# Seven-product block multiplication kept for the gate half only, and the weight sums on VectorE instead of GpSimd, in a two-layer streaming trunk

## The chip, the core and the metric

The kernel runs on one core of a Trainium2 chip. The core has five engines with a queue each: TensorE (PE in the profile; its weight loads are PEld), VectorE (DVE), ScalarE (ACT), GpSimd (POOL) and SyncE (SP), which here only issues DMAs. The metric is the device time of one execution in microseconds (us). The kernel before takes 935.57 us, the median of three runs (935.47 to 936.04). A difference under about 0.2% (2 us) can hardly be told from no change by such a measurement.

## The reference, cut to what is touched

Two residual layers work on a sequence of 512 tokens of width 1024. The first (mLSTM heads beside stick-breaking attention) isn't touched. The second, cut:

```
def odd_layer(x, pre_g, post_g, w_in, pool_w, pool_scale, w_out):
    h = rmsnorm(x, pre_g)
    u = h @ w_in                                  # 512 x 1024 times 1024 x 4096
    p, z = u[..., :2048], u[..., 2048:]           # pooled half, gate half
    pooled = multiscale_pool(p.reshape(B, S, 4, 512))   # trailing mean over 2/4/8/16 tokens, minus the token
    mixed = einsum('bsgc,gce->bsge', pooled, pool_w)    # one 512 x 512 map per group
    y = (mixed.reshape(B, S, 2048) * pool_scale * silu(z)) @ w_out
    return x + rmsnorm(y, post_g)
```

## The kernel before, in words

**Number format.** Every matmul runs in float32r, and each operand is split in two parts, high (`ACT` copies it rounded, line 71) and low (`VectorE` subtracts, line 72). A product of two operands takes three matmuls (`mm3`, lines 95 to 97): high by high, low by high, high by low. So each weight tile costs ScalarE and VectorE one instruction, whatever it is multiplied with. Names that begin with `wh` and `wl` are the two parts of a weight tile.

**The second layer** runs over four channel groups `g` of 512 channels with windows 2, 4, 8, 16. For each group: (1) the pooled half `p`: four channel blocks of 128 (`cur4`), from two weight loads of 1024 x 256; (2) for each of the four blocks the trailing sums by repeated shift and add on VectorE (line 762, once for window 2, up to four times for window 16), a correction of the first tokens on GpSimd (lines 767 and 768, a few columns), the subtraction of the token (line 769), and the split (`pph`, `ppl`); (3) the gate half `z`, two weight loads, with SiLU (`sz`); (4) the map `pool_w`: 48 matmuls into `mx`, and the product with `sz` (line 791).

**Seven products.** Except for `p` of group 0, which is projected directly, every load of 1024 x 256 weights goes through `strassen2`. It sees the weights as four blocks (two halves of the inner dimension by two output blocks) and the transposed hidden state as four blocks too (two halves of the inner dimension by two halves of the sequence). Seven products of such blocks give the four blocks of the result where the plain way takes eight. Each is 4 inner tiles by 3 matmuls, 128 x 256 in shape: 84 matmuls a call. The price is additions: four sums of weight blocks (`s1` to `s4` in the tiles `ws0`, `ws1`; 128 x 512 each), written by GpSimd; four sums of hidden blocks, once for the kernel (`hidden_sums`: `d3`, `d1`, `n2`, `t4`); and partial results that ScalarE copies out of PSUM (`pt`) and VectorE adds (lines 717, 723, 725). The split tiles are `a` (the plain blocks of the first output column), `b` (`s2`, `s1`), `c` (`s3`, `s4`) and `d` (one plain block). `project2` is the plain way: for each of two channel blocks 8 inner tiles by 3 matmuls of 128 x 512, 48 a call, with two split tiles of 128 x 1024.

**What sets the order.** The program is handed to a scheduler that orders each engine's queue by its own estimate of times; each queue then runs strictly in that order. Pools bound how far a stage can run ahead: `wh` and `wl` have four buffers, the raw weights `w32` two, `ws` three, the PSUM tag `pj` two banks (the `psa` of `strassen2`, the `ps` of `project2`), `xa` and `xb` one each (`psb`, `pse`), `ac` two (`mx`).

Of the kernel before, what the change touches and what calls it, by code (L numbers as in the profile page):

```python
# [7 lines left out]
AF = mybir.ActivationFunctionType  # L8
ALU = mybir.AluOpType
# [27 lines left out]
def body(nc, tc, x, pre_g, post_g, w_in, conv, b_i, b_f, hn_g, w_out, w_in_c, pool_w,  # L37
         pool_scale, w_out_c, out):
    V, A, G, T = nc.vector, nc.scalar, nc.gpsimd, nc.tensor
# [4 lines left out]
    with base as base, psum as psum, dram as dram:  # L44
# [25 lines left out]
        def split(src, hi, lo):  # L70
            A.activation(hi, src, AF.Copy)  # L71
            V.tensor_tensor(lo, src, hi.bitcast(F32), op=ALU.subtract)  # L72

        def whl(name):
            return (base.tile([P, WIDE], F32R, tag="wh", bufs=4, name=f"wh_{name}"),
                    base.tile([P, WIDE], F32R, tag="wl", bufs=4, name=f"wl_{name}"))
# [9 lines left out]
        def halves(w, name, into=None):  # L86

            a, n = w.shape[1], w.shape[2]
            wh, wl = (t[:, :a * n].rearrange("p (a n) -> p a n", a=a) for t in (into or whl(name)))
            split(w, wh, wl)  # L90
            return wh, wl
# [94 lines left out]
        def col_load(src, name):  # L186

            w = load(lambda t: [(nc.sync, t, src)], 8, 256, name)
            return [lambda i=i: halves(w[:, :, i * P:i * P + P], f"{name}_{i}") for i in range(2)]
# [6 lines left out]
        def project2(src, name):  # L196
            for i, w in enumerate(col_load(src, name)):
                ps = pj(f"ps_{name}_{i}")
                col_proj(w(), ps)
                yield ps  # L200

        with tc.tile_pool(name="att", bufs=1) as at:
# [386 lines left out]
            for h in range(HA):  # L589
# [7 lines left out]
                for s in range(NB):  # L597
                    t = bc[:, ROW[s]:ROW[s] + P]
# [28 lines left out]
        with tc.tile_pool(name="odd", bufs=1) as od:  # L627
# [60 lines left out]
            def strassen2(src, name, dsts, silu=False):  # L688

                w = load(lambda t: [(nc.sync, t, src)], 8, 256, name)  # L690
                a11, a12, a21, a22 = (w[:, 4 * k:4 * k + 4, m * P:m * P + P]
                                      for m in range(2) for k in range(2))
                sums = [ws(f"ws{i}_{name}") for i in range(2)]
                s1, s2, s3, s4 = sums[0][:, 4:], sums[0][:, :4], sums[1][:, :4], sums[1][:, 4:]
                G.tensor_tensor(s1, a21, a22, op=ALU.add)  # L695
                G.tensor_tensor(s2, s1, a11, op=ALU.add)
                G.tensor_tensor(s3, a11, a21, op=ALU.add)
                G.tensor_tensor(s4, a12, s2, op=ALU.add)
                first = halves(w[:, :, :P], f"{name}_a")
                second = halves(sums[0], f"{name}_b")  # L700
                third = halves(sums[1], f"{name}_c")
                fourth = halves(a22, f"{name}_d")

                def product(ps, wt, k0, b, start, stop):
                    (wh, wl), (bh, bl) = wt, hs[b]
                    for k in range(4):
                        mm3(ps, (wh[:, k0 + k], wl[:, k0 + k]), (bh[:, k], bl[:, k]),
                            start and k == 0, stop and k == 3, skip_group_check=True)

                def part(i): return od.tile([P, 256], F32, tag="part", bufs=4, name=f"pt{i}_{name}")  # L710

                pa, pb, pe = (f(f"ps{n}_{name}")[:, :256] for f, n in ((pj, "a"), (xa, "b"), (xb, "e")))
                t1, t2, t5 = part(1), part(2), part(5)
                product(pa, first, 0, "11", True, True)
                A.activation(t1, pa, AF.Copy)
                product(pb, first, 4, "21", True, True)
                V.tensor_tensor(dsts[0][:, :256], pb, t1, op=ALU.add)
                product(pa, second, 0, "n2", False, True)
                A.activation(t2, pa, AF.Copy)
                product(pe, second, 4, "d1", True, True)  # L720
                A.activation(t5, pe, AF.Copy)
                product(pa, third, 0, "d3", False, True)
                V.scalar_tensor_tensor(dsts[1][:, 256:], pa, -1.0, t5, op0=ALU.mult, op1=ALU.subtract)
                product(pe, third, 4, "22", False, True)
                V.tensor_tensor(dsts[0][:, 256:], pe, t2, op=ALU.add)
                product(pa, fourth, 0, "t4", False, True)
                if silu:
                    act(dsts[0], dsts[0], AF.Silu)
                    act(dsts[1][:, 256:], dsts[1][:, 256:], AF.Silu)
                    act(dsts[1][:, :256], pa, AF.Silu, scale=-1.0)  # L730
                else:
                    A.activation(dsts[1][:, :256], pa, AF.Copy, scale=-1.0)

            for g, w in enumerate(WINDOWS):
                pooled = []
                cur4 = []
                for j in range(4):
                    c = 4 * g + j
                    cur = od.tile([P, 16 + S], F32, tag="win", bufs=6, name=f"p_{c}")
                    G.memset(cur[:, :16], 0.0)  # L740
                    cur4.append(cur)
                wsrc = [w_in_c[0, :, 512 * g + 256 * i:512 * g + 256 * i + 256] for i in range(2)]
                if g == 0:
                    wj = [t() for i in range(2) for t in col_load(wsrc[i], f"p{g}{i}")]
                    for j, n0 in ((j, n0) for n0 in (0, 256) for j in range(4)):
                        ps = pj(f"ps_p{4 * g + j}_{n0}")
                        col_proj(wj[j], ps, n0, n0 + 256)
                        A.activation(cur4[j][:, 16 + n0:16 + n0 + 256], ps[:, n0:n0 + 256], AF.Copy)
                    hidden_sums()
                else:  # L750
                    for i in range(2):
                        strassen2(wsrc[i], f"p{g}{i}", [t[:, 16:] for t in cur4[2 * i:2 * i + 2]])
                for j in range(4):
                    c = 4 * g + j
                    cur = cur4[j]
                    p32 = cur[:, 16:]
                    sh = 1
                    while sh < w:
                        nx = od.tile([P, 16 + S], F32, tag="win", bufs=6, name=f"p_{c}_{sh}")
                        if 2 * sh < w:  # L760
                            G.memset(nx[:, :16], 0.0)
                        V.tensor_tensor(nx[:, 16:], cur[:, 16:], cur[:, 16 - sh:16 + S - sh],  # L762
                                        op=ALU.add)
                        cur, sh = nx, 2 * sh
                    sm = cur[:, 16:]
                    e = w - 1
                    G.tensor_tensor(sm[:, :e], sm[:, :e], invc[:, :e], op=ALU.mult)
                    G.tensor_tensor(sm[:, :e], sm[:, :e], p32[:, :e], op=ALU.subtract)
                    V.scalar_tensor_tensor(sm[:, e:], sm[:, e:], 1.0 / w, p32[:, e:], op0=ALU.mult,
                                           op1=ALU.subtract)  # L770
                    ph = od.tile([P, S], F32R, tag="phi", bufs=5, name=f"pph{c}")
                    pl = od.tile([P, S], F32R, tag="plo", bufs=5, name=f"ppl{c}")
                    split(sm, ph, pl)
                    pooled.append((ph, pl))
                sz = []
                for i in range(2):
                    pair = [od.tile([P, S], F32, tag="sz", bufs=4, name=f"sz{4 * g + 2 * i + j}")
                            for j in range(2)]
                    strassen2(w_in_c[0, :, 2048 + 512 * g + 256 * i:2304 + 512 * g + 256 * i],
                              f"z{g}{i}", pair, True)  # L780
                    sz.extend(pair)
                w4 = load(lambda t: [(nc.sync, t, pool_w[0, g])], 4, 512, f"pw{g}")
                pw = [halves(w4[:, 2 * i:2 * i + 2], f"pw{g}{i}") for i in range(2)]
                for e in range(4):
                    c = 4 * g + e
                    ps = ac(f"mx{c}")
                    for k in range(4):
                        wh, wl = pw[k // 2]
                        mm3(ps, (wh[:, k % 2, e * P:e * P + P], wl[:, k % 2, e * P:e * P + P]),
                            pooled[k], k == 0, k == 3)  # L790
                    V.scalar_tensor_tensor(y32[:, c], ps, psc(c), sz[e], op0=ALU.mult, op1=ALU.mult)
# [44 lines left out]
```

## Time and profile before

| | |
|---|---|
| median of three runs | 935.57 us (935.47 to 936.04) |
| the profiled execution: its own time, its span | 938.04 us, 936.3 us |
| PE busy | 903.9 us, 97% of the span |
| VectorE busy | 603.9 us, 65% |
| ScalarE busy | 503.3 us, 54% |
| GpSimd busy | 170.4 us, 18% |
| mean granted PE clock | 0.981 |

The second layer's groups lie between about 605 and 845 us of the span; then follows the output projection. In the timeline an instruction's duration for PE is that of a pipelined one, from issue to its modelled end; what a matmul costs in a row of them is the distance between two starts. The same holds for VectorE, where a 128 x 512 addition shows 0.68 us and the next one starts 0.60 us after it. A group of instructions is named by line, engine, and output<-inputs, without buffer numbers.

### The profile page before, as it was taken

To read this page: it belongs to the slowest core of one execution; us is meant where nothing else is said; L and a number is where in the kernel's file an instruction comes from. 1 tells how busy PE (TensorE), PEld (TensorE's weight loads), DVE (VectorE), ACT (ScalarE), POOL (GpSimd) and SP (SyncE) were. 2 spreads that over 40 slices of the span, in tenths; PEclk is the share of its full clock that TensorE was granted. 3 is DMA by queue.
4 is the path that set the end of the run, shared out by engine and by line. 5 is a ranking of instruction groups with operands and counts; after the bars stand their busy time and mean duration, and the time that the engine had idled before them with its cause. 6 is when DMAs were issued, how large, how long until landed. Compare 5 with 4: busy or idle time off the path is not lost. (4 is left out here: it accounts for less than half of the span.)

```text
span 936.3 us, 12756 instructions
## 1 busy us (share of the span) xinstructions
PE 903.9 (97%) x4957; PEld 783.1 (84%) x4957; DVE 603.9 (65%) x863; ACT 503.3 (54%) x850; POOL 170.4 (18%) x277
## 2 busy tenths in 40 slices
PE   8999999999999999999999999988989999889997
PEld 6788889888988898898888878888979988868885
DVE  5435555658876673854855556677695887957452
ACT  6436666665776554555467455654434544535331
POOL 2001111101102001010010000065565456510000
PEclk8999999999999999999999999998989999989998
DMA  8232221212222233223312645503122241346331
GB/s 293 89 93 66 71 90 46 90 48 88 80 97 90 85 93 127 91 91 124 96 45 90 225 174 196 169 1 130 51 91 90 91 136 46 114 134 223 109 117 46
DMA packets 67133, 98.97 MB, mean 106 GB/s; under 512 B 2848, under 2 KB 54136, under 8 KB 67072
## 3 DMA queue, kind: packets, MB, share of 16 engines
q1 hardware_dynamic: 65888, 98.08, 32.1%
q8 instruction: 39, 0.64, 0.3%
q10 hardware_dynamic: 1184, 0.08, 0.1%
q14 instruction: 22, 0.18, 0.1%
HBM read 96.02 MB, written 2.13 MB: 105 GB/s over the span
## 5 line engine op out<-in xcount | busy, mean ns | idle before, releaser
L97 PE MATMUL ps_qa<-hTh,wl_qa 128*128 128x512 f32 x128 | 50.3, 393 | 0.0
L95 PE MATMUL ps_qa<-hTh,wh_qa 128*128 128x512 f32 x128 | 50.2, 393 | 0.0
L96 PE MATMUL ps_qa<-hTl,wh_qa 128*128 128x512 f32 x128 | 50.2, 392 | 0.0
L72 DVE TENSOR_TENSOR wl_wo_e<-w_wo_e,wh_wo_e 128x1024 fp32r<-128x1024 f32 x28 | 34.3, 1233 | 23.5 <-ACT wh_wo_e L71 23.3
L71 ACT ACTIVATE wh_wo_e<-w_wo_e 128x1024 fp32r<-128x1024 f32 x28 | 29.4, 1057 | 29.0 <-DMA w_wo_e<-in_w_out_ab 13.6
L540 PE MATMUL op<-wh_wo_e,yl_e 128*128 128x512 f32 x120 | 39.1, 396 | 0.0
L540 PE MATMUL op<-wl_wo_e,yh_e 128*128 128x512 f32 x120 | 39.1, 396 | 0.0
L762 DVE TENSOR_TENSOR p<-p 128x512 f32<-128x512 f32 x40 | 37.9, 955 | 0.1
L540 PE MATMUL op<-wh_wo_e,yh_e 128*128 128x512 f32 x120 | 37.8, 395 | 0.0
L384 POOL TENSOR_TENSOR w<-w,w 128x384 f32<-128x384 f32 (+2 forms) x12 | 10.4, 869 | 144.8 <-DVE pl L72 135.9
L67 ACT ACT_TABLE_LOAD x28 | 35.9, 1283 | 1.3 <-PEq L821 0.8
L97 PE MATMUL psv_va<-wh_va,hTl 128*128 128x256 f32 x128 | 36.1, 282 | 0.0
L95 PE MATMUL psv_va<-wh_va,hTh 128*128 128x256 f32 x128 | 36.1, 282 | 0.0
L96 PE MATMUL psv_va<-wl_va,hTh 128*128 128x256 f32 x128 | 36.1, 282 | 0.0
L695 POOL TENSOR_TENSOR ws_z<-w_z 128x512 f32<-128x512 f32 x8 | 17.8, 2229 | 98.6 <-DVE d1l L72 69.0
L320 DVE SCALAR_TENSOR_TENSOR cv<-u,vecs,cv 128x511 f32<-128x511 f32 (+2 forms) x48 | 35.4, 748 | 0.4
L447 POOL TENSOR_SCALAR_AFFINE_SELECT a<-a 128x128 f32<-128x128 f32 x32 | 12.1, 387 | 126.9 <-DVE a L445 111.3
L72 DVE TENSOR_TENSOR wl_wo_o<-w_wo_o,wh_wo_o 128x1024 fp32r<-128x1024 f32 x20 | 24.3, 1224 | 12.0 <-ACT wh_wo_o L71 12.0
L72 DVE TENSOR_TENSOR wl_qa<-w_qa,wh_qa 128x1024 fp32r<-128x1024 f32 x16 | 19.6, 1222 | 18.4 <-ACT wh_qa L71 18.4
L540 PE MATMUL oq<-wl_wo_o,yh_o 128*128 128x512 f32 x96 | 31.3, 405 | 0.0
L540 PE MATMUL oq<-wh_wo_o,yh_o 128*128 128x512 f32 x96 | 31.3, 404 | 0.0
L71 ACT ACTIVATE wh_wo_o<-w_wo_o 128x1024 fp32r<-128x1024 f32 x20 | 20.9, 1053 | 19.2 <-PE oq L540 8.1
(430 smaller groups left out, 3210.1 us busy)
## 6 DMA issues: line engine op xcount, KB each, us to landing
w_wo_e<-in_w_out_ab SPq DMA_DIRECT2D x14, 1024.0 KB, 4.8
w_wo_o<-in_w_out_c SPq DMA_DIRECT2D x12, 1024.0 KB, 5.0
w_qa<-in_w_in_ab SPq DMA_DIRECT2D x8, 1024.0 KB, 5.0
w_p<-in_w_in_c SPq DMA_DIRECT2D x8, 1024.0 KB, 5.4
w_z<-in_w_in_c SPq DMA_DIRECT2D x8, 1024.0 KB, 5.3
w_qb<-in_w_in_ab SPq DMA_DIRECT2D x4, 1024.0 KB
w_kb<-in_w_in_ab SPq DMA_DIRECT2D x4, 1024.0 KB, 5.0
w_zb<-in_w_in_ab SPq DMA_DIRECT2D x4, 1024.0 KB, 5.0
```

Source lines behind the costliest of these rows:

```text
L67: link(A.preload_act_table_set(TABLE[func]))
L71: A.activation(hi, src, AF.Copy)
L72: V.tensor_tensor(lo, src, hi.bitcast(F32), op=ALU.subtract)
L95: T.matmul(dst, lhsT=ah, rhs=bh, start=first, stop=False, **kw)
L96: T.matmul(dst, lhsT=ah, rhs=bl, start=False, stop=False, **kw)
L97: T.matmul(dst, lhsT=al, rhs=bh, start=False, stop=last, **kw)
L320: V.scalar_tensor_tensor(acc[:, j:], u[:, :S - j], cw(3 - j, c), acc[:, j:], op0=ALU.mult, op1=ALU.add)
L384: G.tensor_tensor(total[:, t0:], total[:, t0:], w[:, t0:], op=ALU.add)
L447: G.affine_select(a[:, t0:t0 + P], a[:, t0:t0 + P], pattern=[[1, P]], base=-1, channel_multiplier=-1, compare_op=ALU.is_ge, fill=0.0)
L540: T.matmul(ps[a][n], lhsT=l[:, ta], rhs=r[:, 0, n * 512:n * 512 + 512], start=(first and l is yh and r is wh), stop=(last and l is yl))
L695: G.tensor_tensor(s1, a21, a22, op=ALU.add)
L762: V.tensor_tensor(nx[:, 16:], cur[:, 16:], cur[:, 16 - sh:16 + S - sh], op=ALU.add)
```

## The change

`p` of groups 1, 2 and 3 is projected by `project2`, like `p` of group 0 though over the whole sequence at once: 48 matmuls of 128 x 512 a call in place of 84 of 128 x 256, six calls in all. ScalarE copies each result from PSUM. The eight calls of `strassen2` for `z` stay. In them the four sums of weights are VectorE instructions now, in another place among the splits. Line numbers behind the change are larger by one (762 becomes 763, 769 becomes 770). The load of weights and all DMAs stay as they are.

```
@@ strassen2
                 sums = [ws(f"ws{i}_{name}") for i in range(2)]
                 s1, s2, s3, s4 = sums[0][:, 4:], sums[0][:, :4], sums[1][:, :4], sums[1][:, 4:]
-                G.tensor_tensor(s1, a21, a22, op=ALU.add)
-                G.tensor_tensor(s2, s1, a11, op=ALU.add)
-                G.tensor_tensor(s3, a11, a21, op=ALU.add)
-                G.tensor_tensor(s4, a12, s2, op=ALU.add)
                 first = halves(w[:, :, :P], f"{name}_a")
+                V.tensor_tensor(s1, a21, a22, op=ALU.add)
+                V.tensor_tensor(s2, s1, a11, op=ALU.add)
                 second = halves(sums[0], f"{name}_b")
+                V.tensor_tensor(s3, a11, a21, op=ALU.add)
+                V.tensor_tensor(s4, a12, s2, op=ALU.add)
                 third = halves(sums[1], f"{name}_c")
                 fourth = halves(a22, f"{name}_d")
@@ the loop over groups
                 else:
                     for i in range(2):
-                        strassen2(wsrc[i], f"p{g}{i}", [t[:, 16:] for t in cur4[2 * i:2 * i + 2]])
+                        for j, ps in enumerate(project2(wsrc[i], f"p{g}{i}")):
+                            A.activation(cur4[2 * i + j][:, 16:], ps, AF.Copy)
```

The first place is VectorE's queue in group 0, around the first `z` load (`w_z_5773`; the second is `w_z_5899`). Rows with - are the queue before, rows with + the queue now, in the order of the queue; L763 and L770 are the old L762 and L769.

```order
 L72 TENSOR_TENSOR n2l<-raw_n_5723,n2h 128x1024
-L762 TENSOR_TENSOR p_1_5744<-p_5477 128x512
-L769 SCALAR_TENSOR_TENSOR p_1_5735<-p_1_5735,p_5475 128x511
+L696 TENSOR_TENSOR ws_z_5775<-w_z_5773 128x512
+L763 TENSOR_TENSOR p_1_5744<-p_5477 128x512
+L770 SCALAR_TENSOR_TENSOR p_1_5735<-p_1_5735,p_5475 128x511
 L72 TENSOR_TENSOR t4l<-raw_t_5729,t4h 128x1024
-L72 TENSOR_TENSOR wl_z_b<-ws_z_5775,wh_z_b 128x1024
-L769 SCALAR_TENSOR_TENSOR p_1_5744<-p_1_5744,p_5477 128x511
-L762 TENSOR_TENSOR p_1_5753<-p_5479 128x512
+L699 TENSOR_TENSOR ws_z_5776<-w_z_5773 128x512
+L697 TENSOR_TENSOR ws_z_5775<-ws_z_5775,w_z_5773 128x512
```

Before, the low part of `b` (`wl_z_b`) stood right behind `t4l`. Now `s1`, `s3`, `s2` stand there, and `wl_z_b` follows as the eighth row behind `s2`:

```order
+L770 SCALAR_TENSOR_TENSOR p_1_5744<-p_1_5744,p_5477 128x511
+L763 TENSOR_TENSOR p_1_5753<-p_5479 128x512
 L72 TENSOR_TENSOR ppl_5741<-p_1_5735,pph_5740 128x512
 L717 TENSOR_TENSOR sz_5771<-psb_z_5798,pt_z_5800 128x256
+L696 TENSOR_TENSOR ws_z_5901<-w_z_5899 128x512
+L700 TENSOR_TENSOR ws_z_5776<-w_z_5773,ws_z_5775 128x512
+L763 TENSOR_TENSOR p_1_5762<-p_5481 128x512
+L72 TENSOR_TENSOR wl_z_b<-ws_z_5775,wh_z_b 128x1024
```

Between them the queue waits at `ppl_5741` for a high part that itself waits for GpSimd's correction.

The second place is VectorE's queue in group 3, from the low part of `c` of the first `z` load to the low part of `a` of the second, which PE needs to go on. Before:

```order
L72 TENSOR_TENSOR wl_z_c<-ws_z_7655,wh_z_c 128x1024
L762 TENSOR_TENSOR p_2_7599<-p_1_7596 128x512
L72 TENSOR_TENSOR ppl_7593<-p_8_7587,pph_7592 128x512
L717 TENSOR_TENSOR sz_7650<-psb_z_7677,pt_z_7679 128x256
L72 TENSOR_TENSOR wl_z_d<-w_z_7652,wh_z_d 128x512
L762 TENSOR_TENSOR p_4_7602<-p_2_7599 128x512
L72 TENSOR_TENSOR wl_z_a<-w_z_7777,wh_z_a 128x1024
```

Now, from the low part of `d` on:

```order
L72 TENSOR_TENSOR wl_z_d<-w_z_7298,wh_z_d 128x512
L763 TENSOR_TENSOR p_8_7269<-p_4_7266 128x512
L763 TENSOR_TENSOR p_1_7278<-p_7098 128x512
L717 TENSOR_TENSOR sz_7296<-psb_z_7323,pt_z_7325 128x256
L770 SCALAR_TENSOR_TENSOR p_8_7269<-p_8_7269,p_7096 128x497
L763 TENSOR_TENSOR p_2_7281<-p_1_7278 128x512
L72 TENSOR_TENSOR wl_z_a<-w_z_7423,wh_z_a 128x1024
```

Before, the second pooled block was still being summed here (`p_2_7599`, `p_4_7602`), and the third and fourth stood behind the last row. Now the third is finished here, and two sums of the fourth stand behind the last row; the four weight sums of the second load stand ahead of the first row.

## Prediction

> **What bounds the kernel now.** First the page: PE is busy for nearly the whole span, so a gain must come from PE's work or from the rest in which it waits or runs slowly.
>
> ```profile
> span 936.3 us, 12756 instructions
> PE 903.9 (97%) x4957; PEld 783.1 (84%) x4957; DVE 603.9 (65%) x863; ACT 503.3 (54%) x850; POOL 170.4 (18%) x277
> ```
>
> Then the stretches of the second layer: the `z` part of group 0, group 1, group 2, group 3, the output projection. Columns: length, busy time of PE, PEld, DVE, ACT and POOL with counts, the granted PE clock, DMA.
>
> ```profile
> 624.60:646.00 21.40, 15.74 (x89) 14.75 (x88) 18.68 (x20) 10.95 (x18) 16.55 (x21) 0.76 0.14 50
> ...
> 658.60:717.30 58.70, 54.34 (x385) 51.78 (x384) 43.38 (x52) 26.13 (x42) 30.70 (x34) 0.94 0.29 90
> 717.30:771.30 54.00, 52.14 (x385) 49.16 (x385) 43.74 (x55) 24.80 (x40) 29.28 (x34) 1.00 0.31 98
> 771.30:840.00 68.70, 61.13 (x411) 56.03 (x410) 52.73 (x63) 31.09 (x49) 33.34 (x35) 0.95 0.31 100
> 840.00:926.00 86.00, 86.00 (x371) 69.27 (x370) 43.80 (x55) 34.09 (x51) 0.00 (x0) 1.00 0.37 123
> ```
>
> What PE loses in a stretch is its idle time plus busy time by the missing share of the clock. Group 1: 58.70 - 54.34 = 4.4, and 54.34 x 0.06 = 3.3, together 7.6 us. Group 2: 1.9. Group 3: 7.6 and 61.13 x 0.05 = 3.1, together 10.6. The sum is 20.1 us. Group 0's `z` part loses 5.7 and 3.8, or 9.5. The last row loses nothing: the projection is pure PE work and moves as a whole. Who ends PE's waits (total, times, longest):
>
> ```profile
> PE psa_z L97 <- DVE wl_z_a L72: 8.1, 4, 2.8
> PE mx L95 <- ACT pph L71: 3.3, 1, 3.3
> PE psb_z L95 <- DVE p L717: 3.3, 3, 1.6
> PE pse_z L95 <- ACT wh_z_b L71: 2.4, 1, 2.4
> ```
>
> Nearly all is VectorE: a low part that comes late, or a PSUM bank (`psb`) that VectorE frees late. The queue that made PE wait in group 3:
>
> ```profile
> 800.25 1.21 DVE L72 TENSOR_TENSOR wl_z_c<-ws_z,wh_z_c 128x1024 fp32r<-128x1024 f32 x1
> 801.39 1.78 DVE L762 TENSOR_TENSOR p<-p 128x512 f32<-128x512 f32 x1
> 803.09 1.78 DVE L72 TENSOR_TENSOR ppl<-p,pph 128x512 fp32r<-128x512 f32 x1
> 804.79 0.41 DVE L717 TENSOR_TENSOR sz<-psb_z,pt_z 128x256 f32<-128x256 f32 x1
> 805.13 1.42 DVE L72 TENSOR_TENSOR wl_z_d<-w_z,wh_z_d 128x512 fp32r<-128x512 f32 x1
> 806.47 1.78 DVE L762 TENSOR_TENSOR p<-p 128x512 f32<-128x512 f32 x1
> 808.18 1.21 DVE L72 TENSOR_TENSOR wl_z_a<-w_z,wh_z_a 128x1024 fp32r<-128x1024 f32 x1
> ...
> 813.22 0.68 DVE L72 TENSOR_TENSOR ppl<-p,pph 128x512 fp32r<-128x512 f32 x1
> ```
>
> There is no idle time in it. A 128x512 instruction is 0.68 in the last row (starts 0.60 apart) and 1.78 above (starts 1.70 apart). In those microseconds GpSimd was at its four weight sums for the second load, one of which is:
>
> ```profile
> 802.58 1.74 POOL L697 TENSOR_TENSOR ws_z<-w_z 128x512 f32<-128x512 f32 x1
> ```
>
> Four of the seven instructions pay 0.74 to 1.1 us for it, 4.0 us together; at 0.60 and 1.14 the queue would take 5.0, not 9.1 us. The whole second layer shows the same in the group's mean of 955 ns:
>
> ```profile
> L762 DVE TENSOR_TENSOR p<-p 128x512 f32<-128x512 f32 x40 | 37.9, 955 | 0.1
> ```
>
> **PE's new work.** From the timeline, a row of matmuls of each width, its first and the matmul behind its last:
>
> ```profile
> 689.50 0.28 PE L97 MATMUL psa_z<-n2h,wl_z_b 128*128 128x256 f32 x1
> ...
> 691.78 0.28 PE L95 MATMUL psb_z<-hTh,wh_z_a 128*128 128x256 f32 x1
> 719.73 0.40 PE L95 MATMUL mx<-pph,wh_pw 128*128 128x512 f32 x1
> ...
> 722.55 0.28 PE L97 MATMUL psb_p<-hTh,wl_p_a 128*128 128x256 f32 x1
> ```
>
> 19 narrow ones in 2.28 us are 0.120 each, 12 wide ones in 2.82 are 0.235. A `strassen2` call is 84 x 0.120 = 10.1 us of PE, `project2` 48 x 0.235 = 11.3: **+1.2 us a call, +7.2 for six**, all on PE and so on the path. This is the change's sure cost.
>
> **VectorE.** A `p` call drops three low parts of 1.14, one of 0.60 and three additions of 0.34 (starts of L717 above), 5.0 us, and takes on two low parts, 2.3: six calls free 16 us. The 32 sums for `z` come onto it. Their form is that of L762, so each costs 0.60 to 1.70; I take 0.60, since what stretched L762 was mainly the sums that leave GpSimd: +19 us. So VectorE's bare work grows by 3 us, while what it lost to GpSimd goes: on L762 alone 40 x (0.955 - 0.68) = 11 us. At GpSimd remain the small corrections and the memsets.
>
> **ScalarE** drops four high parts and four copies a `p` call and takes on two each; in groups 1 to 3 PE waits for it only once, before the last `mx`. The DMAs are the same loads in the same order; no queue gets another one.
>
> **Groups 1 to 3.** What VectorE must do in time is also spread otherwise: with `project2` the four pooled blocks come one after another, 5.6 us apart, so that most of the window sums run under PE's `p` matmuls, where VectorE had gaps. A high part of 128x512 costs ScalarE 0.62:
>
> ```profile
> 800.29 0.62 ACT L71 ACTIVATE wh_z_d<-w_z 128x512 fp32r<-128x512 f32 x1
> ```
>
> I follow the tightest place, group 3, from E, the end of the last `p` matmul. The high part of `d` can only then be rounded, since its buffer is that of the last `p` weights (0.6), then stand `d` 0.60, two sums 1.20, L717 0.34, two more 1.20 and the low part of the second load's `a`, 1.14: done at E+5.1. PE has 48 narrow matmuls before it needs that: E+5.8. So it is 0.7 us in time, with window 16; groups 1 and 2 have one or two sums fewer per block. The `b` and `c` splits and `mx` come later with more to spare. The wait of 3.3 before the last `mx` is that of the fourth block's high part, which stood behind a table load in ScalarE's queue; now it stands 15 rows ahead of it. I count all **20.1 us** as gone. What is late next is this `wl_z_a`.
>
> **Group 0** has no `strassen2` for `p`, and its queue gets longer. The timeline of VectorE, ScalarE, GpSimd and PE there, and one more row of GpSimd from group 3:
>
> ```profile
> 622.49 1.22 DVE L72 TENSOR_TENSOR t4l<-raw_t,t4h 128x1024 fp32r<-128x1024 f32 x1
> 627.32 1.61 DVE L72 TENSOR_TENSOR wl_z_b<-ws_z,wh_z_b 128x1024 fp32r<-128x1024 f32 x1 [3.61 <-ACT wh_z_b L71]
> ```
> ```profile
> 626.23 1.06 ACT L71 ACTIVATE wh_z_b<-ws_z 128x1024 fp32r<-128x1024 f32 x1 [5.41 <-POOL ws_z L696]
> ```
> ```profile
> 617.44 7.41 POOL L695 TENSOR_TENSOR ws_z<-w_z 128x512 f32<-128x512 f32 x1 [68.98 <-DVE d1l L72]
> ...
> 626.15 0.19 POOL L767 TENSOR_TENSOR p<-p,invc 128x1 f32<-128x1 f32 x1
> ```
> ```profile
> 627.34 0.46 PE L95 MATMUL pse_z<-d1h,wh_z_b 128*128 128x256 f32 x1 [2.41 <-ACT wh_z_b L71]
> ...
> 640.45 0.39 PE L97 MATMUL psa_z<-hTh,wl_z_a 128*128 128x256 f32 x1 [2.45 <-DVE wl_z_a L72]
> ```
> ```profile
> 816.98 4.66 POOL L767 TENSOR_TENSOR p<-p,invc 128x15 f32<-128x15 f32 x1 [2.31 <-DVE p L762]
> ```
>
> Before, the first sum sat at GpSimd for 7.41 us, until VectorE's queue paused (622.49 + 1.22). Now the sums stand in VectorE's own queue: `t4l` at 623.1, `s3`, `s2` done at 625.5. But ScalarE's queue has the first block's `pph` ahead of `wh_z_b`, and that needs GpSimd's corrections. If these, like the two long rows, get through only when VectorE pauses, that is at `ppl` (two more instructions, 626.6): corrections 0.5, `pph` 0.6, `wh_z_b` 1.1, PE goes on at 628.8 instead of 627.34; and the low part of `b`, behind `ppl`, L717, three sums, ends at 631.6, so that PE stands twice. From there the queue has no GpSimd sums in it and catches up: I get the second load's `a` at about 640 against 640.45 before, with less half-speed time behind it. **-1 us**, between +4.3 (the delay of `wl_z_b`, passed on whole) and -4 (the late wait and half of the slow clock gone).
>
> **The sum.** +7.2 - 20.1 - 1.0 = **-13.9 us**. The profiled execution took 938.04 us (span 936.3) and would take 924.1; against the median of 935.57 that is **921.7 us**.
>
> **A rule beside the rows.** By the two long GpSimd rows, a small GpSimd instruction waits until VectorE's queue pauses. The Trainium skill, "SBUF — State Buffer", section "Who interferes with whom", says that a VectorE instruction with two SBUF inputs and a GpSimd instruction that reads SBUF exclude each other for one whole instruction, whoever issues first. The 0.68 against 1.78 agrees; the 7.41 and 4.66, longer than any VectorE instruction then running, don't. As a mechanism here: a correction that waits for one instruction alone is through by 623.7, `pph` holds up nothing, `wh_z_b` is ready at 626.5, `wl_z_b` at 630.5, group 0 gains 1.1 more: **920.6 us**.
>
> **The rivals.** (1) The correction gets through at once, as just priced: 920.6. For it speak the 0.19 of 626.15, against it the two long rows. (2) Part of the waits stays. The 0.7 us of group 3 is little; one wait of the size of 2.8 with the slow clock behind it (group 1's 7.6 holds two waits, so some 3 us of slow clock to one) costs 5.8: **927.5 us**. (3) **Slower:** VectorE, which now carries sums, windows and splits, falls behind between `wl_z_d` and the second `wl_z_a` in every group. Against it speaks the 4.0 us that contention leaves; for it, that sums may still meet the corrections at 1.70. With three such waits 17.4 of the 20.1 come back: 935.57 + 7.2 - 1.0 - 2.7 = **939.1**. It decides from 4.6 us lost a group, which is a queue 3.5 longer than I count, or three to four instructions at 1.70. (4) The change frees VectorE without effect, since PE waited for something else: against it the rows, which name VectorE in all but two waits; it would give 935.57 + 7.2 = 942.8.
>
> **How the numbers follow.** The forecast 0.60; rival 1 0.12; rival 2 0.19; rivals 3 and 4 together 0.07; 0.02 for an outcome between. So faster 0.91, same (within 0.2%, about what can be told from no change) 0.02, slower 0.07. The range takes in rival 2 with 1 us more, and below all of group 0's -4 and 2 us of restart time that the busy column hides in some ten waits: 916 to 928.5. The likeliest alone is 918 to 925.
>
> **What would show it.** The changed kernel's stretches of groups 1 to 3: each 54 us long (22.6 + 20.2 + 11.3), PE idle under 1 us, clock 1.00; L763 and the sums at 0.68 to 0.75; no wait for `wl_z_a` in groups 1 to 3; GpSimd under 30 us in the layer. In group 0, PE stops about 4 us before `b`, and again for its low part. The prediction is wrong if waits for `wl_z_a` or `mx` over 2 us remain, or if a sum on VectorE shows 1.2 us or more in the mean.

## The result, and the profile after

The changed kernel takes 919.85 us (median of four runs, 919.13 to 920.03) against 935.52 for the kernel before beside it (four runs, 932.05 to 936.04). The ratio is 0.984, with a 95% interval of 0.982 to 0.986: 15.7 us faster, where the forecast was 13.9. The two profiled executions differ by more, 18.3 us in their spans (936.3 to 918.0), since the profiled execution of before took 938.04 us, longer than any of its four runs; what follows compares these two.

The busy times, as on the page of before:

```profile
span 918.0 us, 12207 instructions
PE 900.2 (98%) x4741; PEld 770.4 (84%) x4741; DVE 581.1 (63%) x865; ACT 491.2 (54%) x826; POOL 76.1 (8%) x221
```

VectorE took over 32 additions, lost what `project2` spares it, and is busy for 22.8 us less (603.9 before). By the prediction's count its bare work grew by 3 us, so by this estimate some 26 us of what it showed before was time lost beside GpSimd. The run with the sums alone (below) gives nearly the same: there VectorE has 56 additions more than before and nothing else, 33.6 us at 0.60 each, and its busy time rises by 6.1 us only (610.0), which is 27.5 us less than the additions would cost.

The stretches of the second layer, by the same columns as before (length; busy time of PE, PEld, DVE, ACT, POOL; granted PE clock; DMA). The first is group 0's `z` part, the others are groups 1, 2 and 3, each cut where the next one's first matmul starts:

```profile
623.98:645.30 21.32, 16.31 (x109) 15.81 (x108) 17.93 (x27) 11.74 (x19) 5.27 (x13) 0.76 0.20 63
655.44:708.83 53.39, 53.39 (x313) 47.10 (x312) 35.75 (x50) 22.14 (x34) 6.10 (x17) 1.00 0.32 99
708.83:762.10 53.27, 53.27 (x314) 47.02 (x313) 37.94 (x54) 21.96 (x34) 6.64 (x20) 1.00 0.31 99
762.10:815.47 53.37, 53.37 (x313) 47.07 (x312) 40.77 (x58) 22.61 (x35) 6.51 (x18) 1.00 0.35 109
```

In groups 1 to 3 PE's busy time equals the length, at full clock: nothing is lost there any more. All that is left are two waits in group 0. PE's waits between 600 and 830 us (total, times, longest), of which the first two matter:

```profile
PE psa_z L95 <- ACT wh_z_b L71: 3.2, 1, 3.2
PE psa_z L97 <- DVE wl_z_b L72: 1.8, 1, 1.8
PE tp_p L179 <- ACT y L184: 0.3, 1, 0.3
```

The window sums (group line, then the first sum of each `z` call by its tile, as minimum, median and maximum in ns) no longer meet a GpSimd sum:

```profile
L763 DVE TENSOR_TENSOR p<-p 128x512 f32<-128x512 f32 x40 | 27.3, 688 | 1.6 <-POOL p L769 0.8
```
```profile
L696 DVE TENSOR_TENSOR ws_z<-w_z x8: 682/692/694, 620.6 to 780.1; 128x512 f32<-128x512 f32 x8
```

Where the 18.3 us of span came from, by stretch; forecasts are the prediction's terms, +2.4 a group for PE's work included (the last matmul of group 0's block `a` starts at 624.65 before and at 623.98 after):

| stretch | forecast | measured |
|---|---|---|
| ahead of group 0's first `b` product | 0 | -0.7 |
| from there to the start of group 1 | -1.0 | 33.95 to 31.46: -2.5 |
| group 1 | -7.6 + 2.4 = -5.2 | 58.70 to 53.39: -5.3 |
| group 2 | -1.9 + 2.4 = +0.5 | 54.00 to 53.27: -0.7 |
| group 3 to the end | -10.6 + 2.4 = -8.2 | 165.0 to 155.9: -9.1 |

The first row's 0.7 us is no effect of the change: it lies in the first 28 us of the span, where PE has the same instructions in both (its 101st matmul starts at 28.29 before and at 27.58 after).

### The profile page after: what moved, and what is told of

It is laid out like the page before. It is cut to its first block, busy times and chain, and to the rows that moved or that the text cites. A ratio compares the mean times of both kernels' runs of the same rounds, so it can differ in the third digit from the quotient of the medians.

```text
span 918.0 us, 12207 instructions
## 1 busy us (share of the span) xinstructions
PE 900.2 (98%) x4741; PEld 770.4 (84%) x4741; DVE 581.1 (63%) x865; ACT 491.2 (54%) x826; POOL 76.1 (8%) x221
## 4 chain that ended last, share of the span: by engine, by line
PE 88%; issue 8%; DVE 1%; POOL 1%; DMA 1%; ACT 0%; SPq 0%; DVEq 0%; POOLq 0%
PE oq L540 10%; PE op L540 5%; PE ps_qa L97 3%; PE ps_qa L96 3%; PE ps_qa L95 3%; PE ps_p L95 2%; PE ps_p L96 2%; PE ps_p L97 2%; PE psa_z L97 2%; PE psv_va L97 2%; PE psv_va L95 2%; PE psv_va L96 2%; PE psa_z L95 2%; PE psa_z L96 2%; PE ps_zb L95 2%
## 5 line engine op out<-in xcount | busy, mean ns | idle before, releaser
L96 PE MATMUL ps_p<-hTl,wh_p 128*128 128x512 f32 (+1 forms) x160 | 55.9, 350 | 0.2 <-DVE hTl L72 0.2
L95 PE MATMUL ps_p<-hTh,wh_p 128*128 128x512 f32 (+1 forms) x160 | 55.7, 350 | 0.0
L97 PE MATMUL ps_p<-hTh,wl_p 128*128 128x512 f32 (+1 forms) x160 | 55.6, 348 | 0.0
L71 ACT ACTIVATE wh_p<-w_p 128x1024 fp32r<-128x1024 f32 x16 | 16.9, 1057 | 46.3 <-issue 26.1
L96 PEld LDWEIGHTS ps_p<-hTl,wh_p 128*128 128x128 f32 x160 | 30.2, 189 | 4.3 <-DVE hTl L72 0.4
L97 PEld LDWEIGHTS ps_p<-hTh,wl_p 128*128 128x128 f32 x160 | 30.2, 189 | 4.1
L95 PEld LDWEIGHTS ps_p<-hTh,wh_p 128*128 128x128 f32 x160 | 30.1, 189 | 4.1
L768 POOL TENSOR_TENSOR p<-p,invc 128x1 f32<-128x1 f32 (+3 forms) x16 | 17.7, 1109 | 162.4 <-DVE p L763 162.3
```

The source lines that it names most:

```text
L95: T.matmul(dst, lhsT=ah, rhs=bh, start=first, stop=False, **kw)
L96: T.matmul(dst, lhsT=ah, rhs=bl, start=False, stop=False, **kw)
L97: T.matmul(dst, lhsT=al, rhs=bh, start=False, stop=last, **kw)
```

## The experiments

Two theories on groups 1 to 3. **C**, contention: a GpSimd addition of 128 x 512 that runs beside VectorE stretches VectorE's instructions, and this alone made the low parts late. **L**, load: what `project2` spares VectorE, and the even spacing of its four blocks, were needed. The runs of one comparison share the kernel before on the same chip (933.9, 933.7 and 934.6 us in the three comparisons).

### The sums alone

```
-                        for j, ps in enumerate(project2(wsrc[i], f"p{g}{i}")):
-                            A.activation(cur4[2 * i + j][:, 16:], ps, AF.Copy)
+                        strassen2(wsrc[i], f"p{g}{i}", [t[:, 16:] for t in cur4[2 * i:2 * i + 2]])
```

> All 14 strassen2 calls stay (p of groups 1 to 3 too), and their weight sums are on VectorE: one part of the change alone. Theory C (contention): PE's waits of before come from GpSimd's sums, which stretch VectorE instructions from 0.60 to 1.70 us; without them the waits of groups 1 to 3 go as they did in the changed kernel, and PE has 7.2 us less work than there: about 912.7 us against the changed kernel's 919.85. Theory L (load and its spread): what cleared the waits is that project2 takes 16 us from VectorE and hands over the pooled blocks one by one. Then VectorE, which in group 3 would have some 49 us of work (14.4 windows and splits of the pooled blocks, 14.8 for z, 15 for p, 5 for the map and its result) in 51 us of PE work, falls behind: waits for wl_z_a or psb_z in groups 2 and 3, 921 us or more. I lean to C in group 1, L in group 3: about 916.

Measured: 921.25 us (920.56 to 921.94), ratio 0.987 (0.985 to 0.988). PE's waits in the second layer:

```profile
PE mx L95 <- ACT pph L71: 4.5, 2, 3.5
PE psa_z L95 <- ACT wh_z_b L71: 3.2, 1, 3.2
PE psa_z L97 <- DVE wl_z_b L72: 2.3, 1, 2.3
```

The waits for `wl_z_a` and `psb` are gone without `project2`, as C says, and groups 1 and 2 are free of waits. One wait grew, at the end of group 3, where the last `mx` needs the high part of the last pooled blocks. So the sums alone bring 12.7 us of the 15.7, although PE has 7.2 us less to do than in the changed kernel: the time came out at L's end of the expectation, for what is lost at the end of group 3 (besides the 4.5 us of waiting, a granted clock of 0.81 from 803 to 821 us).

### The plain product alone

```
 (of before, the sums left on GpSimd)
-                        strassen2(wsrc[i], f"p{g}{i}", [t[:, 16:] for t in cur4[2 * i:2 * i + 2]])
+                        for j, ps in enumerate(project2(wsrc[i], f"p{g}{i}")):
+                            A.activation(cur4[2 * i + j][:, 16:], ps, AF.Copy)
```

> p of groups 1 to 3 by project2, and the weight sums of the eight z calls left on GpSimd: the other part of the change alone. Theory C: VectorE instructions beside the sums still show 1.7 us, and PE's waits for wl_z_a and psb_z stay in the z parts: 928 us or more (before + 7.2 - up to 15). Theory L: VectorE has 16 + 19 us less bare work than in the kernel with sums on VectorE and p by strassen2, so the waits of groups 1 to 3 go although instructions are stretched: 921 or less. Group 0 is as before in both.

Measured: 928.05 us (927.46 to 929.83), ratio 0.994 (0.993 to 0.996). The window sums' group and PE's largest waits:

```profile
L763 DVE TENSOR_TENSOR p<-p 128x512 f32<-128x512 f32 x40 | 38.0, 949 | 1.2
```
```profile
PE psa_z L97 <- DVE wl_z_a L72: 5.4, 4, 2.0
PE psa_z L97 <- DVE wl_z_b L72: 2.9, 1, 2.9
```

The windows stay at 949 ns (955 before) and PE still waits for `wl_z_a` in every group, though for less. `project2` adds 7.2 us to PE and the time falls by 5.9: freeing VectorE does shorten the waits, by some 13 us, but these are largely the same waits that the sums remove. The time lies at the lower end of what C expected, and C's "alone" does not hold: with less work on VectorE the waits shrink even beside GpSimd's sums. The two halves overlap: 12.7 and 5.9 apart, 15.7 together.

### GpSimd's sums given back, twice

The changed kernel, in which GpSimd also repeats the four sums of each `z` call into a row that nobody reads; then the same with the corrections on VectorE, so that nothing that is waited for stands behind the repeats in GpSimd's queue.

```
+                junk = y32[:, 15].rearrange("p (a n) -> p a n", a=4)
+                G.tensor_tensor(junk, a21, a22, op=ALU.add)
+                G.tensor_tensor(junk, junk, a11, op=ALU.add)
+                G.tensor_tensor(junk, a11, a21, op=ALU.add)
+                G.tensor_tensor(junk, a12, junk, op=ALU.add)
```

> The changed kernel, and GpSimd computes the four sums of each z call once more, in the same place of the program, into a part of a buffer that nobody reads before it is overwritten. VectorE's own work is that of the changed kernel; only the contention of before is back. Theory C: windows, splits and sums on VectorE show means of 0.9 us and more instead of 0.7, and waits for wl_z_a come back in groups 1 to 3: 927 us or more. Theory L: the means rise, but the slack takes it up: under 922.

Measured: 957.26 us (956.46 to 958.28), ratio 1.025 (1.023 to 1.027). That is 37 us more than the changed kernel. It is inside C's open "927 us or more" and far above L's 922, but most of the waiting has other names (`psa_z <- ACT pt_z`, 16.2 us, and 9.8 us for `wh_z_b` in group 0), and the window sums' mean is 793 ns, not 900. It leaves open whether the corrections queued at GpSimd were to blame. Hence the second form, on which the order of PE's, ScalarE's and VectorE's queues is the same, instruction for instruction, as in the run without the repeats (the next experiment, 918.38 us):

> The changed kernel with two additions: GpSimd repeats the four weight sums of each z call into a scratch row that nobody reads, and the small corrections L768 and L769 are on VectorE, so that no instruction that anybody waits for stands behind the repeats in GpSimd's queue. VectorE's own work is that of the run with the corrections on VectorE (918.4 us). Theory C (a GpSimd sum beside VectorE stretches VectorE's instructions, and that alone made PE wait for the low parts): the window sums go from 0.68 back to about 0.95 us in the mean, PE waits for wl_z_a again in groups 1 to 3, and the time is 925 to 936. Theory L (the waits went since VectorE had less to do with project2): the windows lengthen or not, PE waits nowhere in groups 1 to 3, and the time stays at 918 to 920.

Measured: 950.39 us (949.40 to 950.53), ratio 1.018 (1.016 to 1.020): **32.0 us** for nothing but additions on GpSimd whose result nobody reads. PE's four largest waits in the second layer add up to 27.8 us, against 4.1 without the repeats, and the run's mean granted clock is 0.977 against 0.991. The repeats also read the raw weights and could have held back the next load; the trace doesn't show that: every wait of a DMA issue between 600 and 860 us ended with a VectorE, PE or DMA instruction, none with one of GpSimd. VectorE's queue in group 1, and GpSimd's beside it:

```profile
682.53 0.69 DVE L701 TENSOR_TENSOR ws_z<-w_z 128x512 f32<-128x512 f32 x1 [1.97 <-DMA w_z<-in_w_in_c]
683.14 2.32 DVE L72 TENSOR_TENSOR wl_z_b<-ws_z,wh_z_b 128x1024 fp32r<-128x1024 f32 x1
685.38 1.78 DVE L702 TENSOR_TENSOR ws_z<-ws_z,w_z 128x512 f32<-128x512 f32 x1
687.08 1.78 DVE L72 TENSOR_TENSOR ppl<-p,pph 128x512 fp32r<-128x512 f32 x1
688.78 0.68 DVE L768 TENSOR_TENSOR p<-p 128x512 f32<-128x512 f32 x1
689.39 1.77 DVE L704 TENSOR_TENSOR ws_z<-w_z 128x512 f32<-128x512 f32 x1
```
```profile
682.64 1.73 POOL L696 TENSOR_TENSOR y<-w_z 128x512 f32<-128x512 f32 x1 [2.78 <-DMA w_z<-in_w_in_c]
684.45 2.16 POOL L697 TENSOR_TENSOR y<-y,w_z 128x512 f32<-128x512 f32 x1
686.69 1.62 POOL L698 TENSOR_TENSOR y<-w_z 128x512 f32<-128x512 f32 x1
...
688.99 1.62 POOL L699 TENSOR_TENSOR y<-w_z,y 128x512 f32<-128x512 f32 x1
```

Four GpSimd additions, four VectorE instructions that are about 1.10 us longer (2.32 for 1.22, 1.78 for 0.68), whatever their own size: 4.4 us. What came of it on ScalarE and PE:

```profile
693.26 0.63 ACT L71 ACTIVATE pph<-p 128x512 fp32r<-128x512 f32 x1 [8.40 <-DVE p L774]
...
698.09 0.38 ACT L720 ACTIVATE pt_z<-psa_z 128x256 f32<-128x256 f32 x1
```
```profile
698.51 0.58 PE L95 MATMUL psa_z<-n2h,wh_z_b 128*128 128x256 f32 x1 [5.50 <-ACT pt_z L720]
```

VectorE's block comes late (`p L774`), ScalarE's queue stands at the `pph` that needs it, and the copy `pt_z` behind that in the same queue, which frees PE's bank, is late with it: 5.5 us in this group. So theory C's cause is shown: GpSimd's additions beside VectorE cost PE this time with no other work changed. Its signature was not the one expected: PE waited for the low part `wl_z_a` for 1.6 us in all, the window sums' mean was 766 ns and not 950, and the time was above the upper end of 936.

### The corrections on VectorE

```
-                    G.tensor_tensor(sm[:, :e], sm[:, :e], invc[:, :e], op=ALU.mult)
-                    G.tensor_tensor(sm[:, :e], sm[:, :e], p32[:, :e], op=ALU.subtract)
+                    V.tensor_tensor(sm[:, :e], sm[:, :e], invc[:, :e], op=ALU.mult)
+                    V.tensor_tensor(sm[:, :e], sm[:, :e], p32[:, :e], op=ALU.subtract)
```

> The changed kernel, with the corrections of the first tokens (two instructions of 1 to 15 columns for each of 16 blocks) on VectorE instead of GpSimd. If GpSimd's correction, which sat 5.85 us in group 0, is what delays the high part of b there, that part is ready at 626.4 minus 0.9 or so, PE's first wait in group 0 falls from 3.2 to about 2 us, and the time to about 918.7. If the sums' own place in VectorE's queue sets it, the time stays at 919.9; if 32 short instructions more are too much for VectorE's slack of 0.7 us in group 3, it rises by up to 3.

Measured: 918.38 us (917.76 to 919.00), ratio 0.984 (0.982 to 0.985). In group 0 the wait for `wh_z_b` fell from 3.2 to 1.8 us, as expected, and the one for `wl_z_b` rose from 1.8 to 2.3; what is left of both is the order of the queue (below). The time alone can't be told from the changed kernel's: the intervals of the two ratios overlap nearly whole.

### Seven products again where nothing waits

Corrections on VectorE; `strassen2` for `p` in groups 1 and 2 alone, then in all three.

```
+                        if g < 3:        # second kernel: in every group
+                            strassen2(wsrc[i], f"p{g}{i}", [t[:, 16:] for t in cur4[2 * i:2 * i + 2]])
+                            continue
```

> Sums and corrections on VectorE; strassen2 for the pooled half of groups 1 and 2, project2 for group 3 alone. Against the run with the corrections on VectorE (918.4 us) PE has 4 x 1.2 = 4.8 us less work. If contention was what made PE wait in groups 1 and 2, no wait comes back there and the time is 913.6 (912.5 to 915). If the freed VectorE time of project2 was needed as well, waits for wl_z_a or psb_z come back in groups 1 and 2, and the time is 917 or more.

> strassen2 for the pooled half everywhere, sums and corrections on VectorE. Without the corrections the same kernel took 921.25 us, with 4.5 us of waiting for the last high part of the pooled blocks (mx <- pph) in group 3 and half clock behind it. If that wait comes from the corrections queued at GpSimd, it goes, and the time is 912 to 915. If it comes from strassen2 itself, which gives its last two blocks only at the end of a call, with four windows each still to be done by VectorE, 3 us or more of it stay, and the time is 918 to 921.

Measured: 913.33 us (912.48 to 914.18), ratio 0.979 (0.977 to 0.980), and 915.55 us (913.93 to 916.13), ratio 0.981 (0.979 to 0.983). PE's waits in the second layer, of the kernel with groups 1 and 2:

```profile
PE psa_z L97 <- DVE wl_z_b L72: 1.9, 1, 1.9
PE psa_z L95 <- ACT wh_z_b L71: 1.8, 1, 1.8
```

and of the one with all three, where the first and the last are those of group 3:

```profile
PE mx L95 <- ACT pph L71: 2.4, 1, 2.4
PE psa_z L97 <- DVE wl_z_b L72: 2.3, 1, 2.3
PE psa_z L95 <- ACT wh_z_b L71: 1.8, 1, 1.8
PE psa_p L95 <- ACT pt_p L719: 0.9, 1, 0.9
```

In groups 1 and 2 nothing comes back, and four calls save 918.38 - 913.33 = 5.05 us, 1.26 a call where the prediction has 1.2. Group 3's two calls should save 2.5 more and cost 2.2. Part of the wait for the last pooled block went with the corrections (4.5 to 2.4 us), part stays; the second run came out between the two theories of its expectation, at neither.

### Group 0's queue in another order

Corrections on VectorE, and in group 0 three constraints of order: `t4`'s low part and `s3` behind `s2`, the window sums behind `wl_z_b` of the first `z` call, whose weights are prepared inside `hidden_sums`.

```
+        def behind(i, k):
+            tc.add_manual_dep(i.ins, table[k].name, NOSYNC, reason="order in group 0")
...
+                behind(V.tensor_tensor(s3, a11, a21, op=ALU.add), "s2")
...
+                        early = prepare(w_in_c[0, :, 2048:2304], "z00")
+                        behind(split(raw[n], *hs[n]), "s2")
...
+                        if g == 0:
+                            behind(step, "b")
```

> Corrections on VectorE, and in group 0 the sums and the b split of the first z call are put ahead of t4's low part and of the window sums in VectorE's queue (order only, no other work). The run with the corrections on VectorE (918.4 us) has two waits of PE left in group 0, 1.8 us for wh_z_b and 2.3 us for wl_z_b, and slower clock behind them. If the order of the queues made these waits, both go: 914 us (913 to 915), and PE never idles over 0.5 us after the first z product. If the sums themselves are too late (they wait for ws buffers or for the load), 1 us or more of waiting stays and the time is 916.5 or more.

Measured: 914.45 us (913.84 to 914.86), ratio 0.980 (0.978 to 0.981). The same stretch of 21 us without and with the order, `z` of group 0:

```profile
624.00:645.00 21.00, 16.95 (x122) 16.53 (x121) 19.48 (x36) 12.68 (x21) 0.56 (x5) 0.84 0.18 60
```
```profile
622.00:643.00 21.00, 19.86 (x156) 18.86 (x156) 21.00 (x39) 12.63 (x22) 0.24 (x3) 1.00 0.17 53
```

With the order VectorE is never idle, PE stands for 1.1 us in place of 4.1, and the clock stays full. The sums were early enough; they stood in the wrong place.

### Both together

> The two gains together: the order of group 0 with the sums and the b split first (914.45 us by itself), and strassen2 for the pooled half of groups 1 and 2 (913.33 by itself, 5.05 below the 918.38 with the corrections on VectorE). If they don't touch each other: 914.45 - 5.05 = 909.4 us (908.5 to 910.5). If the window sums that group 0 puts off make group 1's queue late, a wait of 1 us or more shows in group 1 and the time is 911 or more.

> The same, and in group 3 strassen2 also for the first of the two pooled loads: PE's work falls by 1.2 us more, to 908.2 us, if only the last load's late blocks made the last mx wait. If the first load's blocks are late as well, the wait for pph ahead of mx comes back and the time is 909.5 or more.

Measured: 908.76 us (907.88 to 910.49), ratio 0.973 (0.971 to 0.976), for the order of group 0 with seven products in groups 1 and 2; 909.90 us (909.57 to 910.64), ratio 0.974 (0.973 to 0.976), with the first load of group 3 as well. The first adds up as expected and is the fastest version here, 11.1 us below the changed kernel. The second is the same within the measurement, and no wait for `pph` ahead of `mx` came back. Its 1.2 us of saved work is missing from the time, but not from the trace. The stretch from 10 to 20 us in the two traces, the first kernel above, with the granted clock as the third figure from the end:

```profile
10.00:20.00 10.00, 9.19 (x34) 6.79 (x35) 8.66 (x14) 8.48 (x17) 0.30 (x1) 0.83 0.98 355
```
```profile
10.00:20.00 10.00, 9.27 (x28) 6.63 (x29) 8.74 (x12) 7.40 (x13) 0.31 (x1) 0.66 0.98 354
```

PE has the same instructions there in both, but its 101st matmul starts at 27.30 us in the first kernel and at 28.71 in the second. From that matmul to the end the spans are 880.5 and 879.5 us: the second is 1.0 us shorter. This is one execution of each, so the saving is indicated rather than shown.

## Why the prediction was right, point by point

- **PE +1.2 a call, +7.2:** right. Four calls are worth 5.05 us in the medians, 1.26 each (4.8 in the two spans, 1.2 each).
- **VectorE and contention.** The forecast was 0.60 a sum, 0.68 to 0.75 in the rows, and 0.68 for the windows: 0.682 to 0.694 and 0.688. The 11 us on L762 alone was right (37.9 to 27.3); over all instructions it was some 26 us, by the count above.
- **Groups 1 to 3, 20.1 us gone.** Right as a whole; what the forecast did not separate is which half does it. The runs show that the sums on VectorE suffice in groups 1 and 2, and that `project2`, whose price it also carries, pays in group 3 alone. In the traces these groups with what follows fell by 15.1 us, where the terms give 12.9; the 2.2 us more were not traced. The tightest place was far tighter than forecast. VectorE's queue there, and ScalarE and PE at the same time:

```profile
790.79 0.69 DVE L72 TENSOR_TENSOR ppl<-p,pph 128x512 fp32r<-128x512 f32 x1
791.40 0.68 DVE L72 TENSOR_TENSOR wl_z_d<-w_z,wh_z_d 128x512 fp32r<-128x512 f32 x1
...
794.73 1.22 DVE L72 TENSOR_TENSOR wl_z_a<-w_z,wh_z_a 128x1024 fp32r<-128x1024 f32 x1
```
```profile
790.13 0.63 ACT L71 ACTIVATE pph<-p 128x512 fp32r<-128x512 f32 x1 [3.93 <-POOL p L769]
790.66 0.62 ACT L71 ACTIVATE wh_z_d<-w_z 128x512 fp32r<-128x512 f32 x1
```
```profile
789.98 0.40 PE L97 MATMUL ps_p<-hTh,wl_p 128*128 128x512 f32 x1
...
796.06 0.32 PE L97 MATMUL psa_z<-hTh,wl_z_a 128*128 128x256 f32 x1
```

The last `p` matmul hands over at 790.21 (E). PE wants `wl_z_a` at E+5.85 (forecast E+5.8) and has it at 795.95, E+5.74 (forecast E+5.1): 0.1 us to spare, not 0.7. The step that slipped is `d`: its low part starts at E+1.2 where I had E+0.6. Its high part is late first, done at 791.28 (E+1.07): in ScalarE's queue it stands behind a `pph` that had waited for GpSimd's correction, and I had not put that in. On VectorE the `ppl` of the same block stands ahead as well and adds the last 0.1. Another 0.2 us, and this group would have paid a wait, if a small one; whether it would have grown to the 5.8 us of rival 2 no run shows.

- **Group 0, -1.0:** the mechanism was right, its place in the queue and the size were off; it gave 2.5. The rows of GpSimd, VectorE, ScalarE and PE:

```profile
619.65 5.85 POOL L768 TENSOR_TENSOR p<-p,invc 128x1 f32<-128x1 f32 x1 [71.85 <-DVE p L763]
625.58 0.19 POOL L769 TENSOR_TENSOR p<-p,p 128x1 f32<-128x1 f32 x1
```
```profile
624.76 0.69 DVE L770 SCALAR_TENSOR_TENSOR p<-p,p 128x511 f32<-128x511 f32 x1
625.80 0.69 DVE L763 TENSOR_TENSOR p<-p 128x512 f32<-128x512 f32 x1 [0.35 <-POOL p L769]
...
629.21 1.22 DVE L72 TENSOR_TENSOR wl_z_b<-ws_z,wh_z_b 128x1024 fp32r<-128x1024 f32 x1
```
```profile
625.80 0.63 ACT L71 ACTIVATE pph<-p 128x512 fp32r<-128x512 f32 x1 [2.31 <-POOL p L769]
626.34 1.04 ACT L71 ACTIVATE wh_z_b<-ws_z 128x1024 fp32r<-128x1024 f32 x1
```
```profile
627.43 0.58 PE L95 MATMUL psa_z<-n2h,wh_z_b 128*128 128x256 f32 x1 [3.17 <-ACT wh_z_b L71]
...
630.48 0.58 PE L97 MATMUL psa_z<-n2h,wl_z_b 128*128 128x256 f32 x1 [1.83 <-DVE wl_z_b L72]
```

The correction waits for VectorE's queue to pause, as forecast, and PE stops twice. But the pause comes at 625.45, 1.2 us ahead of the `ppl` I had named: the third block's window sum itself waits for a GpSimd correction (`p L769`). So PE goes on at 627.43, not 628.8, and the low part is there at 630.43, not 631.6. That VectorE would ever wait for GpSimd was missing from my walk.

- **The rivals.** Rival 1 (the correction gets through after one instruction, 920.6) has a time within 0.8 us of the result, but not its mechanism: the correction took 5.85 us and seven VectorE instructions were started meanwhile. Rivals 2 to 4 did not occur. VectorE falling behind in every group, which rival 3 describes, is seen in the run with the repeats, there through GpSimd's additions and not through VectorE's own load.
- **The total.** 13.9 was forecast and 15.7 measured between the medians. In the profiled executions, from which the terms were read, it is 18.3: 0.7 of the difference lies ahead of the change, 1.5 in group 0, 2.2 in groups 1 to 3 and behind. That the medians come within 1.8 us of the forecast is partly luck: the profiled execution of before happened to be 2.5 us longer than its median.

## What to carry to other kernels

A light engine is not free: GpSimd was busy for 18% of the span, and its additions delayed the engine that everybody waited for. Look for one form of instruction with two durations (0.68 and 1.78 us) and see what ran beside the long one; work given to the busier engine can cost it far less than its own length (33.6 us of additions, 6.1 us of busy time in the run with the sums alone). After such a repair price each half of a change anew, place by place: the plain product cost 1.26 us a call and paid in one group of three, and the order of a queue ahead of a stalled product was worth 4 us with no work changed.

## What the runs showed of the hardware

- In the rows of the repeats a GpSimd addition of 128 x 512 adds the same 1.10 us to a VectorE instruction of 512 and of 1024 columns. The two engines took turns there: GpSimd's 684.45 + 2.16 ends at 686.61, and VectorE's instruction issued at 685.38 ends 0.55 us later, at 687.16. With this the Trainium skill agrees ("SBUF — State Buffer", section "Who interferes with whom"): one engine has the shared port for a whole instruction while the other blocks.
- The small correction in group 0 did not get its turn: issued at 619.65, it ended with VectorE's pause at 625.45, and VectorE paused only because it had to wait for the correction behind this one in GpSimd's queue. A rule by which it waits for one instruction doesn't give that. What decides between taking turns and waiting for a pause is open; no run here separates it.
- Two idle times of PE of 1.8 and 2.3 us went with a mean clock of 0.84 over 21 us (the slow rows stand behind the second idle time, with starts 0.213 us apart from 629.75 to 634.8, before and behind them 0.120); without them it was 1.00. In the same 21 us PE started 156 matmuls in place of 122; 34 more, at 0.120 us or more each, are some 4 us, and the median fell by 3.9.
- From 10 to 20 us of the span, where the compared kernels have the same PE instructions, the granted clock was 0.66 in one execution (28.71 us for the start of PE's 101st matmul) and 1.00 in another (25.67 us, the kernel with seven products in all three groups). So two single executions can differ by 3 us ahead of everything that was changed.
